# Layer 1: recurrent heads as a pipeline in slots, between the levels of one head the scan of the head before and the projections of the next

## The chip, the core and the metric

The kernel runs on one core of a Trainium2 chip. Five engines work from queues of their own, each in order: PE (matrix products; its weight loads are listed as PEld), DVE and ACT (element-wise work), POOL (a little arithmetic, and output DMAs) and SP (most input DMAs). The metric is the device time of one execution in microseconds, and lower is better. Before the change it was 3807.29 us, the median of three runs (3806.28 to 3817.9).

## The reference

The model has two layers over 1024 latent tokens and 256 context tokens, with 1024 features. Layer 0 (neighbourhood attention beside an mLSTM) isn't touched by the change. Layer 1 is a gated linear recurrence with 16 heads that runs forward and backward over the tokens. Cut to what matters:

```
q, f_fwd, f_bwd, i, z = split(h @ w_in)           # per head 128 columns of each
f = lb + (1 - lb) * sigmoid(f_pre)                # decay, per key feature; k = 1 - f
for d in (forward, backward):                     # i is the value
    S = final state over the 256 context tokens
    for each chunk of tokens:                     # b = running sum of log f in the chunk
        o += (q * exp(b)) @ S + (pairs t >= s: q_t . exp(b_t - b_s) k_s) @ i
        S = exp(b_last) * S + (k * exp(b_last - b))^T @ i
y = (rms(o_fwd + o_bwd) * h_norm * silu(z)) @ w_out
x = x + gate * y
```

All of it is in 32-bit floats. The large products are made of three matmuls with operands that were split into a high and a low part.

## The kernel before

**Stages of layer 1.** First `q_plain` and `q_seven` compute the values `i` and the gated `z` of all heads for the latent tokens (eight blocks of 256 columns) and write them to DRAM (`vzd`). Then the 16 heads follow, in a loop at the end of `build`. Then the output projection (`out_ahead`, `out_tile`).

**One head**, in the order in which the program is written:

- `hg_intra`. From the decay F and the query q come K = 1 - F and Q = q F, for two halves of 512 tokens. Then `hg_level` runs seven times on each half: blocks of 1, 2, 4 to 64 tokens are joined in pairs. A level copies the keys that it needs (`gksel`, ACT, L1022), makes 4 products of 128 x 128 (L1031, eight matmuls, since a 32-bit product takes two), puts the result into the matrix A under a mask (L1041, DVE), and multiplies K and Q by the decay of the neighbouring block (L1049, DVE, four times). At level 0 A is made anew (L1037), and `hg_diag` adds the diagonal. At the end K is transposed into `gkn` (L1006, L1008).
- `hg_vz` loads v and z of the head (SP), projects the values of the context tokens (24 matmuls of 256 columns, L120 to L122) and transposes them (L947).
- `hg_ctx` makes the two states after the context: running products of the decay (L960, L961, DVE), keys, transposes (L967), products (L974).
- `hg_scan` takes eight chunks of 128 tokens: seven backward states (L1071, L1073), then for each chunk three products into the accumulator bank (L1083 to L1085) and the next forward state (L1088, L1090); after four chunks each the norm and the gate (L1099, POOL for the inverse root, L1103).
- `hg_proj` of the **next** head: for both directions the context tokens and two halves of the latents through the decay weights (24 matmuls each; sigmoid L786 on ACT, affine step L787 on DVE), then q (L795, L796).
- `hg_y` transposes the output and writes it to DRAM (POOL).

**What sets the order.** Loops are unrolled in Python. A planner orders the instructions of each engine ahead of time: of what it holds ready at a moment it takes what stands first in the program, so what comes later in the program fills in where earlier work waits. Tiles are given out by tag from a fixed number of buffers, and an instruction waits until a buffer of its tag is free. What matters here: `gF` (decay of a half) has two buffers, and level 0 is the last to read it; `gFc` (decay of the context) has one; `gEc` has one, and both the context values of `hg_vz` and the running products of `hg_ctx` take it; `gq` has two, for the two halves of q and the keys of `hg_ctx`; the split weights have four slabs, two for each block of 128 columns. Of the eight PSUM banks two serve projections (`mm`), two transposes (`tr`), three small products (`s`), and one the scan (`acc`).

Of the kernel before, what the change touches and what calls it, by code (L numbers as in the profile page):

```python
# [18 lines left out]
P = 128  # L19
# [24 lines left out]
class Prog:  # L44
# [727 lines left out]
    def hg_proj(self, h, pool):  # L772
        nc, a = self.nc, self.a
        st = {}
        col = lambda i: a["wc"][:, i * 2048 + h * P : i * 2048 + (h + 1) * P]
        lb, olb = self.lb[:, 0, h : h + 1], self.lb[:, 1, h : h + 1]
        F = [self.t(pool, [P, 2, 512], F32, "gF", 2) for _ in range(2)]
        Fc = self.t(pool, [P, 2, CTX], F32, "gFc", 1)
        todo = [(d, t0, n) for d in range(2) for t0, n in ((LAT, CTX), (512, 512), (0, 512))]
        w = [None, None]  # L780
        for d, t0, n in todo:
            w[d] = w[d] or self.wring([col(1 + d)], P)
# [3 lines left out]
            nc.scalar.activation(dst, ps, AF.Sigmoid)  # L786
            nc.vector.tensor_scalar(out=dst, in0=dst, scalar1=olb, scalar2=lb, op0=ALU.mult, op1=ALU.add)  # L787
        q = {}
        w = self.wring([col(0)], P)
        for t0 in (512, 0):  # L790
            ps = self.ps("mm", [P, 512])
            self.proj_tr(ps, w, 0, t0, 512)
            q[t0 // 512] = self.t(pool, [P, 512], F32, "gq", 2)
            sg = self.t(pool, [P, 512], F32, "gsg", 1)
# [39 lines left out]
    def q_raw(self, pool, j):  # L834
        nc, raw = self.nc, {}
        for n in ("11", "21", "12", "22"):
# [95 lines left out]
    def hg_vz(self, h, st, pool):  # L932
        nc, a = self.nc, self.a
        v = self.t(pool, [P, NT, P], F32, "gv", 2)
        z = self.t(pool, [P, NT - 2, P], F32, "gz", 2)
        for t, i in ((v, 0), (z, 1)):
            nc.sync.dma_start(
                out=t[:, 0:8, :], in_=self.vzd[i, :, h * P : (h + 1) * P].rearrange("(c p) f -> p c f", p=P)
            )
# [8 lines left out]
        nc.scalar.copy(v[:, 8:10, :], pt)  # L948
        st["v"], st["z"] = v, z


    def hg_ctx(self, st, pool):
        nc = self.nc
        Fc, v = st["Fc"], st["v"]
        E = self.t(pool, [P, 2, CTX], F32, "gEc", 1)
        k = self.t(pool, [P, 2, CTX], F32, "gq", 2)
# [5 lines left out]
        nc.vector.tensor_scalar(out=k, in0=Fc, scalar1=-1.0, scalar2=1.0, op0=ALU.mult, op1=ALU.add)  # L962
        nc.vector.tensor_tensor(out=k, in0=k, in1=E, op=ALU.mult)
        p = self.ps("tr", [P, 4, P])
        for d in range(2):
            for j in range(2):
                nc.tensor.transpose(p[:, 2 * d + j, :], k[:, d, j * P : (j + 1) * P], self.ident)  # L967
        kn = self.t(pool, [P, 4, P], F32, "gknc", 1)
        nc.scalar.copy(kn, p)
        S = []  # L970
        for d in range(2):
            u = self.ps("s", [P, P])
            for j in range(2):
                nc.tensor.matmul(u, lhsT=kn[:, 2 * d + j, :], rhs=v[:, 8 + j, :], start=(j == 0), stop=(j == 1))  # L974
# [500 lines left out]
```

## Time and profile before

| | |
|---|---|
| median of three runs | 3807.29 us |
| profiled execution | 3808.09 us, span 3806.3 us |
| mean granted PE clock | 0.982 |
| busy: PE / DVE / ACT / POOL | 94% / 63% / 39% / 14% of the span |
| value and gate products of layer 1 | about 1975 to 2306 us from the span's start |
| heads of layer 1 | 2313 to about 3664 us |
| from K of one head to K of the next | 80 to 84 us, 64.8 for the first |
| output projection | to the end |

The profile's page gives for each engine the time in which it was busy. PE's matmuls overlap, so the duration of one is longer than the distance to the next. In the tables by stretch stands the busy time of each engine between two points of time, and behind it the number of instructions. A row of the order of time has the start, the time taken, engine, line, operation, written and read tiles, and in square brackets the idle time before it and what ended it. A row of groups has count, busy time and mean duration in ns, then the idle time before. A row of waits has who waited for whom, the total in us, how many times, and the longest.

### The profile page before, as it was taken

The page shows a single profiled execution, that of the slowest core. Times are in us where ns is not written, and L with a number is a line of the kernel's source. Part 1 is how long each engine was busy: PE and PEld are TensorE (multiplying, and loading weights), DVE is VectorE, ACT ScalarE, POOL GpSimd, SP SyncE. Part 2 cuts the span into 40 slices and gives each one's busy share as a digit, 9 for nine tenths or more (in the row PEclk, how much of TensorE's full clock was granted, in tenths as well). Part 3 has the DMA queues.
Part 4 walks back from the last instruction along what each step waited for, and adds up shares of the span by engine and source line. Part 5 has one row for each costly group of instructions (what it writes and reads, how often), then busy time and mean ns, then how long its engine had stood idle before and what let it go on. Part 6 is the DMA issues. An engine that isn't in the chain of part 4 may idle for free.

```text
span 3806.3 us, 65773 instructions
## 1 busy us (share of the span) xinstructions
PE 3575.2 (94%) x24618; PEld 3221.9 (85%) x24618; DVE 2383.2 (63%) x6294; ACT 1477.0 (39%) x3459; POOL 514.8 (14%) x880
## 2 busy tenths in 40 slices
PE   8999999999999999988879999899999899998989
PEld 5889999999999999976559998778888778887777
DVE  5546676666546556545448665766667766667763
ACT  5545555554434334333343332333333333333431
POOL 2222222222111122010011220000000000000000
PEclk9999999999999999999999999999999999999999
DMA  6522323232343343246233322111111111111244
GB/s 211 171 72 77 87 83 86 68 84 80 86 152 99 118 138 112 72 153 201 91 108 104 109 92 83 43 39 45 50 51 51 39 39 46 50 54 47 89 152 128
DMA packets 363054, 348.26 MB, mean 91 GB/s; under 512 B 31128, under 2 KB 315992, under 8 KB 362608
## 3 DMA queue, kind: packets, MB, share of 16 engines
q1 hardware_dynamic: 324560, 243.66, 21.9%
q0 software_dynamic: 38176, 100.40, 7.6%
q8 instruction: 195, 3.19, 0.3%
q14 instruction: 123, 1.01, 0.1%
HBM read 267.70 MB, written 76.08 MB: 90 GB/s over the span
## 4 chain that ended last, share of the span: by engine, by line
PE 62%; issue 14%; DVE 11%; DMA 7%; POOL 3%; ACT 2%; SPq 0%; POOLq 0%; ACTq 0%; DVEq 0%
PE mm L120 13%; PE mm L122 13%; PE mm L121 13%; DMA wraw<-yd 3%; DVE gQ L1049 3%; DVE gA L1041 3%; DVE gK L1049 2%; PE s L1031 2%; PE acc L677 2%; PE tr L657 2%; POOL vzd L883 2%; PE s L470 1%; PE acc L461 1%; PE mm L731 1%; PE mm L733 1%
## 5 line engine op out<-in xcount | busy, mean ns | idle before, releaser
L122 PE MATMUL mm<-wh,hl 128*128 128x256 f32 x2560 | 749.3, 293 | 0.3 <-DVE hl L253 0.3
L120 PE MATMUL mm<-wh,hh 128*128 128x256 f32 x2560 | 746.8, 292 | 0.0
L121 PE MATMUL mm<-wl,hh 128*128 128x256 f32 x2560 | 745.6, 291 | 0.0
L120 PE MATMUL mm<-hh,wh 128*128 128x512 f32 (+1 forms) x1344 | 487.6, 363 | 24.6 <-ACT gFc L786 16.8
L122 PEld LDWEIGHTS mm<-wh,hl 128*128 128x128 f32 x2560 | 488.8, 191 | 11.2 <-issue 4.1
L120 PEld LDWEIGHTS mm<-wh,hh 128*128 128x128 f32 x2560 | 489.0, 191 | 7.7 <-issue 1.4
L121 PEld LDWEIGHTS mm<-wl,hh 128*128 128x128 f32 x2560 | 489.0, 191 | 7.1 <-issue 0.8
L121 PE MATMUL mm<-hl,wh 128*128 128x512 f32 (+1 forms) x1344 | 485.3, 361 | 0.0
L122 PE MATMUL mm<-hh,wl 128*128 128x512 f32 (+1 forms) x1344 | 485.0, 361 | 0.0
L1031 PE MATMUL s<-gQ,gksel 128*128 128x128 f32 x1536 | 240.9, 303 | 74.4 <-ACT gksel L1022 61.6
L120 PEld LDWEIGHTS mm<-hh,wh 128*128 128x128 f32 x1344 | 255.7, 190 | 61.6 <-ACT gFc L786 19.7
L71 ACT CAST wh<-wraw 128x512 fp32r<-128x512 f32 x278 | 171.1, 620 | 335.6 <-PE mm L121 242.9
L1031 PEld LDWEIGHTS s<-gQ,gksel 128*128 128x128 f32 x1536 | 212.4, 201 | 95.9 <-ACT gksel L1022 73.7
L72 DVE TENSOR_TENSOR wl<-wraw,wh 128x512 fp32r<-128x512 f32 x278 | 189.9, 689 | 152.1 <-ACT wh L71 149.7
L122 PEld LDWEIGHTS mm<-hh,wl 128*128 128x128 f32 x1344 | 255.7, 190 | 34.6
L121 PEld LDWEIGHTS mm<-hl,wh 128*128 128x128 f32 x1344 | 255.8, 190 | 33.7
L731 PE MATMUL mm<-woh,yh 128*128 128x512 f32 x524 | 216.2, 413 | 55.6 <-ACT yh L71 38.2
L1022 ACT COPY gksel<-gK 128x512 f32<-128x512 f32 x224 | 148.7, 664 | 234.5 <-DVE gA L1041 94.3
L733 PE MATMUL mm<-woh,yl 128*128 128x512 f32 x524 | 215.5, 412 | 0.4 <-DVE yl L72 0.4
L732 PE MATMUL mm<-wol,yh 128*128 128x512 f32 x524 | 211.3, 404 | 0.0
L731 PEld LDWEIGHTS mm<-woh,yh 128*128 128x128 f32 x524 | 101.1, 193 | 90.7 <-ACT yh L71 55.9
L71 ACT CAST yh<-wraw 128x512 fp32r<-128x512 f32 x144 | 86.7, 619 | 217.4 <-DMA wraw<-yd 123.8
(432 smaller groups left out, 7900.5 us busy)
## 6 DMA issues: line engine op xcount, KB each, us to landing
wraw<-yd SPq DMA_DIRECT2D x144, 256.0 KB
wraw<-in_wc_dram SPq DMA_DIRECT2D x132, 256.0 KB
wraw<-in_wab_dram SPq DMA_DIRECT2D x112, 256.0 KB
md<-ev POOLq DMA_DIRECT2D x100, 256.0 KB, 2.8
adar<-in_wada_dram POOLq DMA_DIRECT2D x32, 512.0 KB, 4.6
b<-in_wc_dram SPq DMA_DIRECT2D x64, 256.0 KB
vzd<-qo POOLq DMA_DIRECT2D x128, 128.0 KB, 2.2
adar<-in_wada_dram SPq DMA_DIRECT2D x16, 512.0 KB
```

What stands on the lines that cost most here:

```text
L71: nc.scalar.copy(hi, x)
L72: nc.vector.tensor_tensor(out=lo, in0=x, in1=hi.bitcast(F32), op=ALU.subtract)
L120: mm(ps, lhsT=lh(k), rhs=rh(k), start=(k == 0), stop=False)
L121: mm(ps, lhsT=lh(k), rhs=rl(k), start=False, stop=False)
L122: mm(ps, lhsT=ll(k), rhs=rh(k), start=False, stop=(k == nk - 1))
L731: mm(ps, lhsT=yh[:, k, :], rhs=w.h(kk), start=(kk == 0), stop=False)
L732: mm(ps, lhsT=yh[:, k, :], rhs=w.l(kk), start=False, stop=False)
L733: mm(ps, lhsT=yl[:, k, :], rhs=w.h(kk), start=False, stop=(kk == 8 * len(qs) - 1))
L1022: nc.scalar.copy(ksel.rearrange("p (b s i) -> p b s i", s=2, i=h), pick(K))
L1031: nc.tensor.matmul(pa[:, c, :].rearrange("p (b s i) -> p b s i", s=2, i=h), lhsT=ksel[:, c * P : (c + 1) * P], rhs=qp[:, c * nbc : (c + 1) ...
L1041: nc.vector.copy_predicated(A, self.lmask[:, lev - 1, :].unsqueeze(1).to_broadcast([P, 4, P]), pa)
L1049: nc.vector.tensor_tensor(out=t[:, i, :, s, :], in0=t[:, i, :, s, :], in1=bc(tot), op=ALU.mult)
```

## The change

- **Slots.** `hg_intra` calls eight slots: slot 0 before level 0, slot i + 1 behind level i. `hg_scan` no longer runs, it returns its seven parts (three with backward states, four with two chunks each), and `hg_parts` (formerly `hg_proj`) returns the projections in parts. During the levels of head h the slots hold the scan of head h - 1 (slots 0 to 6), the context step of head h (slot 1), the projections of head h + 1 (decay in slots 2 to 5, context tokens last in slots 3 and 5, q in slots 6 and 7), the output of head h - 2 (slot 2) and the loads of v and z of head h (slot 4).
- **Tiles.** The context values and keys get tags of their own (`gvT`, `gvc`), `hg_ctx` makes its keys in place, and Q, A and the last decay products get four buffers, since two heads are alive.
- **Engines.** The affine step of the decay goes from DVE to ACT; half of the `gkn` copies goes from ACT to DVE; at level 6 two ACT copies of blocks stand in for the predicated copy; the copy of Q ahead of the product moves from level 6 to level 0.
- **Before the heads.** The first decay weights of head 0 are loaded while the value pool is still open. In `q_plain` only one half of the first weights is loaded early, and eight accumulators are kept open: first the products of the upper half of the features for all eight row tiles, then those of the lower half.

The diff, with `...` where lines are left out:

```diff
...
-    def hg_proj(self, h, pool):
+    def hg_parts(self, h, pool, w=None):
...
+        st, w, F = {"q": {}}, w or {}, {}
+
+        def weights(i):
+            if i not in w:
+                w[i] = self.wring([col(i)], P)
+            return w[i]
+
+        def f(d, t0, n):
+            if t0 not in F:
+                F[t0] = self.t(pool, [P, 2, n], F32, "gFc" if t0 == LAT else "gF", 1 if t0 == LAT else 2)
             ps = self.ps("mm", [P, n])
-            self.proj_tr(ps, w[d], 0, t0, n)
-            dst = Fc[:, d, :] if t0 == LAT else F[t0 // 512][:, d, :]
+            self.proj_tr(ps, weights(1 + d), 0, t0, n)
+            dst = F[t0][:, d, :]
             nc.scalar.activation(dst, ps, AF.Sigmoid)
-            nc.vector.tensor_scalar(out=dst, in0=dst, scalar1=olb, scalar2=lb, op0=ALU.mult, op1=ALU.add)
...
+            nc.scalar.activation(dst, dst, AF.Identity, scale=olb, bias=lb)
+            st["F"] = [F.get(0), F.get(512)]
+
+        def q(t0):
             ps = self.ps("mm", [P, 512])
...
-            nc.scalar.activation(sg, ps, AF.Sigmoid)
-            nc.vector.tensor_tensor(out=q[t0 // 512], in0=sg, in1=ps, op=ALU.mult)
-        return dict(F=F, Fc=Fc, q=q)
+            self.proj_tr(ps, weights(0), 0, t0, 512)
+            t = st["q"][t0 // 512] = self.t(pool, [P, 512], F32, "gq", 2)
+            nc.scalar.activation(t, ps, AF.Sigmoid)
+            nc.vector.tensor_tensor(out=t, in0=t, in1=ps, op=ALU.mult)
+
+        def c():
+            st["S"] = self.hg_ctx(F[LAT], weights(3), pool)
+
+        todo = [[]] + [[(f, d, 512, 512)] if k == 0 else [(f, d, 0, 512), (f, d, LAT, CTX)] for d in range(2) for k in range(2)]
+        todo += [[(q, 512)], [(q, 0)]]
+        st["c"] = c
+        return st, [[lambda x=x: x[0](*x[1:]) for x in xs] for xs in todo]
...
-            w = early if early and not z else [self.q_form(raw, f"{k}{z + 1}") for k in (1, 2)]
-            for c in (4, 0):
-                for i in range(4):
-                    ps = self.ps("sa", [P, 256])
-                    for k in range(2):
-                        self.q_mul(ps, self.q_h(c + i, k), w[k], k == 0, k == 1)
-                    self.q_out(pool, c + i, j, z, ps)
+            ps = []
+            w = early if not z else self.q_form(raw, "12")
+            for i in [4, 5, 6, 7, 0, 1, 2, 3]:
+                ps.append((i, self.q_ps()))
+                self.q_mul(ps[-1][1], self.q_h(i, 0), w, True, False)
+            w = self.q_form(raw, "22" if z else "21")
+            for i, p in ps:
+                self.q_mul(p, self.q_h(i, 1), w, False, True)
+                self.q_out(pool, i, j, z, p)
...
     def hg_vz(self, h, st, pool):
...
+        for n, i in (("v", 0), ("z", 1)):
+            st[n] = self.t(pool, [P, 8, P], F32, "g" + n, 2)
+            self.nc.sync.dma_start(
+                out=st[n], in_=self.vzd[i, :, h * P : (h + 1) * P].rearrange("(c p) f -> p c f", p=P)
             )
-        w = self.wring([a["wc"][:, 3 * 2048 + h * P : 3 * 2048 + (h + 1) * P]], P)
+
+    def hg_ctx(self, Fc, w, pool):
+        nc = self.nc
         ps = self.ps("mm", [P, CTX])
         self.proj_tr(ps, w, 0, LAT, CTX)
-        vT = self.t(pool, [P, CTX], F32, "gEc", 1)
+        vT = self.t(pool, [P, CTX], F32, "gvT", 1)
...
-        nc.scalar.copy(v[:, 8:10, :], pt)
-        st["v"], st["z"] = v, z
...
+        v = self.t(pool, [P, 2, P], F32, "gvc", 1)
+        nc.scalar.copy(v, pt)
         E = self.t(pool, [P, 2, CTX], F32, "gEc", 1)
-        k = self.t(pool, [P, 2, CTX], F32, "gq", 2)
...
-        nc.vector.tensor_scalar(out=k, in0=Fc, scalar1=-1.0, scalar2=1.0, op0=ALU.mult, op1=ALU.add)
-        nc.vector.tensor_tensor(out=k, in0=k, in1=E, op=ALU.mult)
+        nc.vector.scalar_tensor_tensor(out=E, in0=Fc, scalar=1.0, in1=E, op0=ALU.subtract, op1=ALU.mult)
...
         kn = self.t(pool, [P, 4, P], F32, "gknc", 1)
-        nc.scalar.copy(kn, p)
+        nc.scalar.activation(kn, p, AF.Copy, scale=-1.0)
...
-            s = self.t(pool, [P, P], F32, f"gS{d}", 10 if d else 2)
+                nc.tensor.matmul(u, lhsT=kn[:, 2 * d + j, :], rhs=v[:, j, :], start=(j == 0), stop=(j == 1))
+            s = self.t(pool, [P, P], F32, f"gSc{d}", 2)
...
-    def hg_intra(self, st, pool):
+    def hg_intra(self, st, pool, slots):
...
-            Q = self.t(pool, [P, 2, n], F32, "gQ", 2)
+            Q = self.t(pool, [P, 2, n], F32, "gQ", 4)
...
-            A = self.t(pool, [P, 4, P], F32, "gA", 2)
+            A = self.t(pool, [P, 4, P], F32, "gA", 4)
...
+        slot(0)
         for lev in range(7):
             for hf in (1, 0):
                 self.hg_level(hv[hf], lev, pool)
             if lev == 0:
                 for hf in (1, 0):
                     self.hg_diag(hv[hf], st["q"][hf], pool)
+            slot(lev + 1)
...
-                nc.scalar.copy(k_, p)
+                (nc.vector.tensor_copy if d else nc.scalar.copy)(k_, p)
                 H["kn"].append(k_)
...
-        if lev == 6:
+        if lev == 0:
...
+        elif lev == 6:
+            nc.scalar.copy(A[0:64, :, 64:128], pa[0:64, :, 64:128])
+            nc.scalar.copy(A[64:128, :, 0:64], pa[64:128, :, 0:64])
         else:
             nc.vector.copy_predicated(A, self.lmask[:, lev - 1, :].unsqueeze(1).to_broadcast([P, 4, P]), pa)
...
-    def hg_scan(self, h, st, halves, S, pool):
+    def hg_scan(self, st, halves, pool):
...
+        S = {0: st["S"][0]}
+        sb = {7: st["S"][1]}
+        o4 = {}
+
+        def state(d, c, old, tag, bufs):
...
+            nc.tensor.matmul(u, lhsT=H["kn"][d][:, c % 4, :], rhs=v[:, c, :], start=True, stop=True)
+            s = self.t(pool, [P, P], F32, tag, bufs)
...
+            return s
+
+        def back(c):
+            sb[c - 1] = state(1, c, sb[c], "gS1", 9)
+
+        def ahead(c):
...
-            nc.tensor.matmul(o, lhsT=H["Q"][:, 1, cs], rhs=Sf, start=False, stop=True)
+            nc.tensor.matmul(o, lhsT=H["Q"][:, 1, cs], rhs=S[c], start=False, stop=True)
...
+                S[c + 1] = state(0, c, S[c], "gS0", 2)
+            if c % 4 == 3:
...
+        do = lambda f, *cs: [lambda c=c: f(c) for c in cs]
+        return [do(back, 7, 6, 5), do(back, 4, 3), do(back, 2, 1)] + [do(ahead, c, c + 1) for c in (0, 2, 4, 6)]
...
-                early = []
-                for k in range(2):
-                    rows = a["wc"][k * 512 : (k + 1) * 512, 3 * 2048 : 3 * 2048 + 256]
-                    early.append(self.wblock(self.wp, "w", [rows], 4, 256, op, ring=self.slabs))
+                early = self.wblock(self.wp, "w", [a["wc"][0:512, 3 * 2048 : 3 * 2048 + 256]], 4, 256, op, ring=self.slabs)
...
-                self.nq = 0
+                self.nq = -1
...
+                    first = [a["wc"][:, 2048 : 2048 + P]]
+                    early = {1: self.wblock(self.wp, "w", first, KD, P, [pool, 4, "b11"], ring=self.slabs)}
...
-                st = self.hg_proj(0, pool)
+                st, parts = self.hg_parts(0, pool, early)
+                for part in sum(parts, []):
+                    part()
+                scan, done = [], [None, None]
                 for h in range(16):
-                    hv = self.hg_intra(st, pool)
-                    self.hg_vz(h, st, pool)
-                    S = self.hg_ctx(st, pool)
-                    self.hg_scan(h, st, hv, S, pool)
-                    done = st
-                    if h < 15:
-                        st = self.hg_proj(h + 1, pool)
-                    self.hg_y(h, done, pool, self.yd2)
+                    nxt, parts = self.hg_parts(h + 1, pool) if h < 15 else (None, [])
+                    slots = [[] for _ in range(8)]
+                    for i, x in enumerate(scan):
+                        slots[i] += x
+                    slots[1] += [st["c"]]
+                    for i, x in enumerate(parts):
+                        slots[i + 1] += x
+                    if h > 1:
+                        slots[2].append(lambda h=h, st=done[0]: self.hg_y(h - 2, st, pool, self.yd2))
+                    slots[4].append(lambda h=h, st=st: self.hg_vz(h, st, pool))
+                    hv = self.hg_intra(st, pool, slots)
+                    scan = self.hg_scan(st, hv, pool)
+                    done, st = [done[1], st], nxt
+                self.hg_y(14, done[0], pool, self.yd2)
+                for part in sum(scan, []):
+                    part()
+                self.hg_y(15, done[1], pool, self.yd2)
```

More of the change, by code (lines that the diff above doesn't have):

```diff
@@ L835, in q_raw @@
         nc, raw = self.nc, {}
-        for n in ("11", "21", "12", "22"):
+        for n in ("11", "21", "12", "22")[j == 0 :]:
             c0 = (3 if n[1] == "1" else 4) * 2048 + j * 256
@@ L984, in hg_intra, with slot @@
         hv = {}
+        def slot(i):
+            for part in slots[i]:
+                part()
         for hf in (1, 0):
@@ L1097, in hg_scan @@
-            jk = self.t(pool, [P, P], F32, "gjk", 1)
-            for i in range(4):
-                nc.scalar.activation(jk, o4[:, i, :], AF.Square, accum_out=ss[:, i : i + 1])
-            self.rsqrt(ss, ss, 1.0 / P)
-            for i in range(4):
-                zi = z[:, c - 3 + i, :]
-                nc.vector.scalar_tensor_tensor(
-                    out=zi, in0=o4[:, i, :], scalar=ss[:, i : i + 1], in1=zi, op0=ALU.mult, op1=ALU.mult
-                )
+                S[c + 1] = state(0, c, S[c], "gS0", 2)
@@ new lines, in ahead @@
+            if c % 4 == 3:
+                ss = self.t(pool, [P, 4], F32, "gss", 2)
+                jk = self.t(pool, [P, P], F32, "gjk", 1)
+                for i in range(4):
+                    nc.scalar.activation(jk, o4[0][:, i, :], AF.Square, accum_out=ss[:, i : i + 1])
+                self.rsqrt(ss, ss, 1.0 / P)
+                for i in range(4):
+                    zi = z[:, c - 3 + i, :]
+                    nc.vector.scalar_tensor_tensor(
+                        out=zi, in0=o4[0][:, i, :], scalar=ss[:, i : i + 1], in1=zi, op0=ALU.mult, op1=ALU.mult
+                    )
```

51 lines of the change are left out of this document (6 added, 45 removed).

## The prediction

> **What bounds the kernel now.** I read the page first (engine shares, then the chain that ended last), then a table of busy time by stretch, then the order of time inside one head, then the waits.
>
> ```profile
> PE 3575.2 (94%) x24618; PEld 3221.9 (85%) x24618; DVE 2383.2 (63%) x6294; ACT 1477.0 (39%) x3459; POOL 514.8 (14%) x880
> PE 62%; issue 14%; DVE 11%; DMA 7%; POOL 3%; ACT 2%; SPq 0%; POOLq 0%; ACTq 0%; DVEq 0%
> ```
>
> PE is the engine to look at, but its 94% hides holes: matmuls overlap, so a sparse PE also looks busy. The stretches below show them. Columns: length, then busy time (and instructions) of PE, PEld, DVE, ACT, POOL, then the granted clock, DMA share and GB/s. 2403 to 3541 is the stretch of 14 heads of layer 1 (heads 1 to 14), 81.3 us each; 2729 to 2810 is one head.
>
> ```profile
> 2403.00:3541.00 1138.00, 1033.70 (x6414) 918.38 (x6413) 782.23 (x1960) 372.92 (x798) 51.20 (x84) 0.98 0.15 46
> 2729.00:2810.00 81.00, 73.54 (x460) 65.77 (x459) 55.90 (x141) 26.63 (x57) 3.65 (x6) 0.98 0.16 46
> 2655.00:2699.00 44.00, 44.00 (x287) 40.20 (x285) 26.52 (x66) 13.82 (x34) 3.65 (x6) 1.00 0.27 78
> 2699.00:2721.00 22.00, 14.51 (x108) 12.51 (x106) 21.91 (x57) 8.40 (x15) 0.00 (x0) 1.00 0.00 1
> 3596.00:3638.00 42.00, 42.00 (x240) 36.63 (x239) 30.56 (x69) 19.14 (x34) 0.12 (x1) 1.00 0.25 76
> ```
>
> In a head, 44 us are solid (PE 44.00 of 44) and then 22 us aren't: PE 14.51, DVE 21.91 of 22. In those 22 us the levels run alone:
>
> ```profile
> 2705.60 0.97 PEld L1031 LDWEIGHTS s<-gQ,gksel 128*128 128x128 f32 x8 [0.98 <-ACT gksel L1022]
> 2705.64 1.13 PE L1031 MATMUL s<-gQ,gksel 128*128 128x128 f32 x8 [0.82 <-ACT gksel L1022]
> 2706.09 0.71 DVE L1041 COPY_PREDICATED gA<-glm,s 128x512 f32<-128x512 uint8 x1
> 2706.70 0.73 DVE L1049 TENSOR_TENSOR gQ<-gQ,gT 128x256 f32<-128x256 f32 x2
> 2706.84 0.62 ACT L1022 COPY gksel<-gK 128x512 f32<-128x512 f32 x1 [1.33 <-DVE gA L1041]
> 2707.37 0.74 DVE L1049 TENSOR_TENSOR gK<-gK,gT 128x256 f32<-128x256 f32 x2
> 2707.55 0.97 PEld L1031 LDWEIGHTS s<-gQ,gksel 128*128 128x128 f32 x8 [0.98 <-ACT gksel L1022]
> ```
>
> A half-level comes every 1.95 us (2705.60 to 2707.55), paced by DVE; PE has 0.97 us of loads in it and stands 0.98. No projection fills the gap, and this is why:
>
> ```profile
> 2719.47 0.38 PE L947 MATMUL tr<-ident,gEc 128*128 128x128 f32 x2
> 2719.91 0.68 DVE L960 TENSOR_TENSOR_SCAN gEc<-gFc,gzero 128x255 f32<-128x255 f32 x1
> 2720.51 0.67 DVE L961 TENSOR_TENSOR_SCAN gEc<-gFc,gzero 128x255 f32<-128x255 f32 x1
> 2721.20 0.66 ACT L786 ACTIVATE gFc<-mm 128x256 f32<-128x256 f32 x2 [0.68 <-DVE gEc L961]
> 2721.64 0.50 PE L120 MATMUL mm<-hh,wh 128*128 128x512 f32 x1 [1.13 <-ACT gFc L786]
> ACT gFc L786 <- DVE gEc L961: 12.8, 14, 1.3
> PE mm L120 <- ACT gFc L786: 15.7, 14, 1.1
> ```
>
> The next head's projection starts with its context part, whose tile gFc has one buffer. This head's context step still has to read that buffer (L960, L961); it writes gEc, a single buffer that holds the context values until their transposes (L947), and those run only when the levels are over. So the projection restarts behind the levels, in each of 14 heads (the last two rows: total us, times, longest).
>
> **PE's work in a head.** I price a matmul by the distance between starts in solid stretches, since its duration overlaps its neighbours.
>
> ```profile
> 2722.44 0.40 PE L120 MATMUL mm<-hh,wh 128*128 128x512 f32 x1
> 2725.87 0.39 PE L120 MATMUL mm<-hh,wh 128*128 128x512 f32 x1
> 2318.24 0.28 PE L120 MATMUL mm<-hh,wh 128*128 128x256 f32 x1
> 2318.96 0.28 PE L120 MATMUL mm<-hh,wh 128*128 128x256 f32 x1
> 2353.91 1.30 PEld L1031 LDWEIGHTS s<-gQ,gksel 128*128 128x128 f32 x8
> ```
>
> 15 matmuls of 512 columns lie between the first two: 0.229 us each. Six of 256 between the next two: 0.12. Of 128: eight loads in 0.97 us, the last lasting about 0.19, so 0.78 / 7 = 0.111; at level 0, where Q is read with a stride, 1.11 / 7 = 0.159 (last row). By the code a head has 144 matmuls of 512 (six projections of 24), 72 of 256 (three of 24) and 242 of 128, together 458 (the table counts 460 in 81 us). That is 144 x 0.229 + 72 x 0.12 + 242 x 0.111 = 33.0 + 8.6 + 26.9 = 68.5 us, plus 16 x 0.048 = 0.8 at level 0 now. PE idles 81.3 - 69.3 = 12 us a head, 168 us in 14 heads, nearly all in the levels.
>
> **The change, part by part.**
>
> Order. The context step moves to slot 1 with tiles of its own (gvT, gEc), so gFc is free two slots before the next head writes it (slot 3). Scan chunks of the head before, context step and projections of the next get places between levels. No matmul is added. What blocked the filler goes; after level 0 the two gF buffers free, and 39 us of projection (33.0 and two of 2.9) plus the scan can fill. How solid will PE be? The nearest row is 3596 to 3638, the last head, where the output projection is the filler among the levels; its largest groups:
>
> ```profile
> L732 PE MATMUL mm<-wol,yh 128*128 128x512 f32 x43 | 17.1, 399 | 0.0
> L1031 PE MATMUL s<-gQ,gksel 128*128 128x128 f32 x80 | 10.7, 276 | 0.0
> ```
>
> There are 131 matmuls of 512 (43, 43, 42 in the three lines of that sum, and 3) and 109 of 128 (80 here, 13 and 16): 30.0 + 12.1 = 42.1 us of work in 42. So it can be all but full. I take 97%, some 2 us a head for the seams between the parts: 68.5 / 0.97 = 70.6 us, 10.7 less a head, 14 x 10.7 = 150 us. Bounds: 99% gives 69.2 (169 us); below, no gain at all and a loss (rivals).
>
> Engines. The rows for what moves between them:
>
> ```profile
> L787 DVE TENSOR_SCALAR gF<-gF,lb 128x512 f32<-128x512 f32 x56 | 30.5, 545 | 107.4 <-ACT gF L786 107.4
> L786 ACT ACTIVATE gF<-mm 128x512 f32<-128x512 f32 x56 | 33.3, 595 | 20.9 <-PE mm L122 20.9
> L1114 ACT ACTIVATE gyt<-tr,hnc 128x512 f32<-128x512 f32 x28 | 19.3, 689 | 112.7 <-PE tr L1112 112.7
> L1041 DVE COPY_PREDICATED gA<-glm,s 128x512 f32<-128x512 uint8 x168 | 123.9, 738 | 4.5 <-PE s L1031 3.9
> L1008 ACT COPY gkn<-tr 128x512 f32<-128x512 f32 x56 | 31.6, 585 | 38.7 <-PE tr L1006 38.6
> L1037 DVE TENSOR_TENSOR gA<-s,glm 128x512 f32<-128x512 f32 x28 | 19.4, 692 | 50.4 <-PE s L1031 50.4
> ```
>
> The decay's affine step leaves DVE (4 x 0.545 a head, and two narrow ones, about 0.4) for ACT: a per-partition operand costs 0.689 - 0.595 = 0.094, so two make about 0.78 for 512 columns and 0.6 for 256 (estimates). Two of four gkn copies go to DVE (about 0.69 from PSUM, as L1037; ACT saves 0.585). At level 6 a predicated copy of 0.738 per half becomes two ACT copies of about 0.4. The Q copy moves from level 6 to level 0, one per half as before. The context's two DVE passes become one. DVE: 55.9 - 3.0 + 1.4 - 1.5 - 0.4 = 52.4 us a head. ACT: 26.6 + 4.3 - 1.2 + 1.6 + 0.5 = 31.8. Both stay under 70.6, so I charge nothing: the cover is PE's own work, and were it gone, DVE's 52.4 would be the floor. If ACT were late, gksel and then PE's levels wait behind it.
>
> DMA queues. Each head's gv and gz loads move on SP to slot 4, ahead of the next weights; gz waits for the output transposes of two heads earlier (slot 2), and weights queue behind. DMA share is 0.15, a whole slot lies between: 0. The output DMA of a head goes out on POOL one head later, and the scan's inverse root (POOL, slots 4 and 6) queues behind it, with the one accumulator bank behind that; POOL is busy 51.20 of 1138, so 0, at most 4 us at the end, where head 14's write now stands ahead of head 15's.
>
> Start of the heads, and the first value/gate block:
>
> ```profile
> 2309.45 1.47 SPq L100 DMA_DIRECT2D wraw<-in_wc_dram  x3
> 2312.35 1.28 ACT L71 CAST wh<-wraw 128x512 fp32r<-128x512 f32 x2 [5.99 <-DMA wraw<-in_wc_dram]
> 2313.03 0.58 PE L120 MATMUL mm<-hh,wh 128*128 128x256 f32 x1 [7.63 <-ACT wh L71]
> 2314.47 0.41 PE L122 MATMUL mm<-hh,wl 128*128 128x256 f32 x1
> 2316.18 0.37 PE L121 MATMUL mm<-hl,wh 128*128 128x256 f32 x1
> 1987.66 0.58 PE L863 MATMUL sa<-wh,hh 128*128 128x256 f32 x1 [4.62 <-ACT qo L878]
> ```
>
> The first decay weights are now loaded (two DMAs on SP) and split under the last gate product, so the 7.63 us wait goes. What is late next: the second weights, which can only be asked for where the first are now (2309.45, ready 2313); three projections, 13.8 us, cover that. Behind the wait 256-column matmuls start 0.21 apart (2314.47 to 2316.18, eight) instead of 0.12 up to 2316.4: 1.5 us more. Gain 9. In the first block only the k-half "11" is early; "21" must be loaded once the old pool is gone, near 1987, and takes 2.9 us from issue to cast (2309.45 to 2312.35) while PE already stands 4.62 there. Eight accumulators instead of four give PE no more to do before that. I charge 2 us, between -1 (two splits fewer ahead of the last row tile) and 5.
>
> The Trainium skill, "TensorE: Matmul & The Clock Gate", Part 1, says that an idle window of about 3.4 us halves PE's clock until a busy one has passed. The trace agrees: 2313.03 to 2316.4 is 3.4 us at the slow pace. By that rule the gain from closing the wait is 7.6 + 1.7 = 9.3 us, against my 9 from rows.
>
> The last head keeps its shape: levels among output filler, its scan exposed. 1 us from level 0.
>
> **Sum.** 150 + 9 - 2 + 1 = 158. The profiled execution took 3808.1 us (span 3806.3 and 1.8 around it), 0.8 above the median: 3808.1 - 158 = 3650, and against the median of 3807.3, 3649.
>
> The Trainium skill, "Perfetto Trace Analysis", section "Identifying the Most-Contended Engine", judges PE by weight-load busy time, not matmul busy time. Here that speaks against my price: a head's loads take 65.77 us, the solid stretches read 40.20 of 44 (91%), so by that measure a solid head takes 65.77 / 0.914 = 72.0, the gain is 14 x 9.3 + 8 = 138 and the time 3670. The trace agrees that matmul busy time says little: 44.00 of 44, and still 73.54 of 81 over a whole head.
>
> **Rivals.**
>
> A, a hole at each head's start. Level 0 needs fresh K, Q, A, sums and diagonal on DVE, eight or nine passes near 0.69 per half, about 13 us for two; PE has level 0 and diagonal (3.6), the context step (72 x 0.12 is 8.6 in all, 2.9 of it here, and 14 x 0.111) and five backward states there, some 9 us, and the next projection waits for gF. For: DVE waits 50.4 us before L1037 today. Against: the last q projection (5.5 us) lies there too. Price 4 to 6 us a head: 75.6, gain 14 x 5.7 + 8 = 88, time 3720.
>
> B, slower: queue order. PE takes its queue in order. Now 14 scan states join 14 half-levels between parts, each ending in a PE-DVE or PE-ACT-PE round; where the order written out leaves too little work between, the 0.98 us gap of today's half-level stays. It decides at 81.3 - 68.5 = 12.8 us, 13 such gaps of 28, plus a half more for the 9 us at the start. With 21 exposed: 89.1 us, 14 x 7.8 - 8 = 101 more, 3909. Against: 2655 to 2699 holds such scan states already, and PE is solid.
>
> C, the change doesn't do what it says: another single buffer (gF until level 0, or the four weight slabs) blocks the filler as gFc does. Only the start is gained: 3800. Against: both are freed a slot or more before use.
>
> **How the numbers follow.** Forecast (97% to 99%, down to 74 us a head) 0.66, A 0.17, C 0.04, B 0.13. Time 3649, own range 3620 to 3700. Leaving out B, C and the worse half of A leaves 3615 to 3735, about 0.75 to 0.8. About 0.3% (11 us) is what a measurement can tell from no change: faster 0.83, same 0.04, slower 0.13.
>
> **What would show it.** Right: distance between heads near 70.6 us; no PE wait on gFc; context transposes early in a head; PE near 99% busy, weight loads near 90% in the heads, PE's matmul count unchanged; DVE near 52 of 70; no 7.6 us wait before the first head. Wrong: PE waits on gksel, gS or gA of 0.5 to 1 us at many half-levels (B); one hole of several us per head near L1037 (A); waits on another tile's buffer at 22 us per head (C).

## The result, and the profile after

The changed kernel takes 3548.44 us (median of 4 runs, 3547.46 to 3549.17), the kernel before 3806.78 on the same chip: a ratio of 0.9315, 95% interval 0.9298 to 0.9333. That is 258 us less; I had forecast 158 less, and my own range began at 3620. The profiled execution took 3547.46 us with a span of 3545.7.

The engine shares and the chain that ended last, on the page of the changed kernel:

```profile
PE 3473.2 (98%) x24618; PEld 3175.5 (90%) x24618; DVE 2311.4 (65%) x6182; ACT 1550.8 (44%) x3587; POOL 538.4 (15%) x880
PE 83%; issue 8%; DMA 4%; DVE 2%; POOL 1%; ACT 1%; SPq 0%; POOLq 0%; ACTq 0%; DVEq 0%
```

The number of matmuls is the same (24618). What left the chain is above all DVE (11% to 2%) and "issue" (14% to 8%).

Busy time by stretch in the changed kernel (columns as in the prediction): the last part of layer 0's output stage, then heads 1 to 14, then one head.

```profile
1843.00:1913.00 70.00, 70.00 (x351) 58.98 (x350) 43.56 (x113) 39.01 (x104) 8.00 (x16) 1.00 0.41 125
2339.00:3301.00 962.00, 962.00 (x6403) 875.38 (x6402) 719.49 (x1851) 436.04 (x896) 71.33 (x80) 1.00 0.18 53
2613.00:2682.00 69.00, 69.00 (x461) 62.76 (x461) 51.78 (x135) 31.70 (x67) 5.36 (x6) 1.00 0.18 54
```

The heads are solid: PE 962.00 of 962. Inside a head, a piece of the context step, a half-level and a projection now stand next to each other. The timeline of the changed kernel (start, length, instruction, and in brackets the idle time before it; line numbers are those of the kernel shown, so the product of a level, L1031 before, is L1041 here, and the sigmoid and the affine step are L789 and L790):

```profile
2641.90 0.40 PE L122 MATMUL mm<-hh,wl 128*128 128x512 f32 x1
...
2642.13 1.06 PE L978 MATMUL s<-gvc,gknc 128*128 128x128 f32 x8
2642.33 0.60 ACT L789 ACTIVATE gF<-mm 128x512 f32<-128x512 f32 x1 [2.94 <-PE mm L122]
...
2642.95 0.48 PE L120 MATMUL mm<-hh,wh 128*128 128x512 f32 x1
2642.96 0.81 ACT L790 ACTIVATE gF<-gF,lb 128x512 f32<-128x512 f32 x1
...
2643.72 0.40 PE L120 MATMUL mm<-hh,wh 128*128 128x512 f32 x1
...
2643.95 0.77 PE L1041 MATMUL s<-gQ,gksel 128*128 128x128 f32 x5
```

No PE row has a bracket: the idle time of 0.8 to 1 us at each half-level is gone. Now ACT waits for PE (2.94). The last row is cut off by the end of the view, after five of its eight matmuls.

I cut both spans at the same four events: the last norm of layer 0, the last write of values and gates, the first K of head 1, and the first K of head 15.

| stretch | before, us | after, us | difference | forecast |
|---|---|---|---|---|
| to the last norm of layer 0 | 1978.8 | 1912.9 | -65.9 | in the next row |
| value and gate stage | 328.3 | 330.4 | +2.1 | +2 |
| to the first K of head 1 | 95.9 | 95.9 | 0 | -9 |
| heads 1 to 14 | 1138.0 | 961.4 | -176.6 | -150 |
| from the first K of head 15 to the end | 265.3 | 245.1 | -20.2 | -1 |

So the profiled execution lies 103 us below my sum, for three reasons: 66 us in a stage that the forecast did not look at, 27 us more in the heads, and 10 us more around them (20 against 9 and 1).

### The profile page after: what moved, and what is told of

The parts are those of the page before. It is cut to its first block, busy times and chain, and to the rows that moved or that the text cites. A ratio compares the mean times of both kernels' runs of the same rounds, so it can differ in the third digit from the quotient of the medians.

```text
span 3545.7 us, 65436 instructions
## 1 busy us (share of the span) xinstructions
PE 3473.2 (98%) x24618; PEld 3175.5 (90%) x24618; DVE 2311.4 (65%) x6182; ACT 1550.8 (44%) x3587; POOL 538.4 (15%) x880
## 4 chain that ended last, share of the span: by engine, by line
PE 83%; issue 8%; DMA 4%; DVE 2%; POOL 1%; ACT 1%; SPq 0%; POOLq 0%; ACTq 0%; DVEq 0%
PE mm L122 14%; PE mm L120 14%; PE mm L121 14%; PE s L1041 6%; PE acc L677 2%; PE tr L657 2%; PE mm L731 2%; PE mm L732 2%; PE mm L733 2%; PE sa L873 2%; PE sa L872 2%; PE sa L874 2%; PE s L470 1%; PE acc L461 1%; PE s L1086 1%
## 5 line engine op out<-in xcount | busy, mean ns | idle before, releaser
L731 PE MATMUL mm<-woh,yh 128*128 128x512 f32 x524 | 210.6, 403 | 16.3 <-issue 10.1
L733 PE MATMUL mm<-woh,yl 128*128 128x512 f32 x524 | 209.5, 400 | 0.0
L1041 PE MATMUL s<-gQ,gksel 128*128 128x128 f32 x1536 | 199.8, 276 | 0.0
L1041 PEld LDWEIGHTS s<-gQ,gksel 128*128 128x128 f32 x1536 | 192.4, 191 | 7.0
L145 POOL TENSOR_SCALAR gss<-gss 128x4 f32<-128x4 f32 x32 | 16.6, 518 | 968.0 <-ACT gjk L1111 968.0
L1062 DVE TENSOR_TENSOR gQ<-gQ,gT 128x256 f32<-128x256 f32 x384 | 143.1, 413 | 28.0 <-PE s L1041 28.0
```

The source lines that it names most:

```text
L731: mm(ps, lhsT=yh[:, k, :], rhs=w.h(kk), start=(kk == 0), stop=False)
L733: mm(ps, lhsT=yl[:, k, :], rhs=w.h(kk), start=False, stop=(kk == 8 * len(qs) - 1))
L1041: nc.tensor.matmul(pa[:, c, :].rearrange("p (b s i) -> p b s i", s=2, i=h), lhsT=ksel[:, c * P : (c + 1) * P], rhs=qp[:, c * nbc : (c + 1) ...
L1062: nc.vector.tensor_tensor(out=t[:, i, :, s, :], in0=t[:, i, :, s, :], in1=bc(tot), op=ALU.mult)
```

## Experiments

Each time is a median; "before" is the kernel before on the same chip. It took 3803.78 to 3806.78 us in the four sets of runs, so a difference of some 3 us between times of different sets says nothing.

### Where do 66 us of layer 0 come from?

In the kernel before, this is the same part of the output stage, 1853 to 1979, by busy time:

```profile
1853.00:1979.00 126.00, 100.42 (x432) 71.40 (x431) 54.14 (x127) 48.33 (x119) 8.66 (x19) 0.97 0.28 87
```

and by its waits (total us, times, longest):

```profile
ACT yh L71 <- DMA wraw<-yd: 49.0, 24, 3.7
PEld mm L731 <- ACT yh L71: 34.3, 24, 3.6
PE mm L731 <- ACT yh L71: 24.9, 24, 3.1
```

PE waits for ACT, and ACT for the rows of y. The timeline of the kernel before shows the round:

```profile
1900.85 0.62 ACT L71 CAST yh<-wraw 128x512 fp32r<-128x512 f32 x1 [3.60 <-DMA wraw<-yd]
...
1901.52 0.50 PE L731 MATMUL mm<-woh,yh 128*128 128x512 f32 x1 [0.90 <-ACT yh L71]
1902.21 0.36 SPq L718 DMA_DIRECT2D wraw<-yd  x1
...
1905.05 0.62 ACT L71 CAST yh<-wraw 128x512 fp32r<-128x512 f32 x1 [1.01 <-DMA wraw<-yd]
```

The next rows are asked for (1902.21) only when the last ones have been split, and are split themselves 2.8 us later: one staging buffer in use, though the tag `wraw` has three. The theory: the second early half of the first weights ("21") was requested ahead of this stage. Its two pieces sat in two of the three buffers, since their destinations, the slabs of tag `w`, were held by the last two pieces of the output weights until the stage's end. The timeline has both ends of this. The request (the last two of its three DMAs) and the split:

```profile
1780.82 1.60 SPq L100 DMA_DIRECT2D wraw<-in_wc_dram  x3
1974.60 1.31 ACT L71 CAST wh<-wraw 128x512 fp32r<-128x512 f32 x2 [2.71 <-PE mm L733]
```

For more than 190 us the two pieces held their staging buffers, until PE's last products of the stage (L733).

**The first block alone.** The kernel before with only the edit of the first value/gate block: one early half, and `q_raw`, `q_plain` and the first value of `nq` as in the changed kernel.

```diff
-                early = []
-                for k in range(2):
-                    rows = a["wc"][k * 512 : (k + 1) * 512, 3 * 2048 : 3 * 2048 + 256]
-                    early.append(self.wblock(self.wp, "w", [rows], 4, 256, op, ring=self.slabs))
+                early = self.wblock(self.wp, "w", [a["wc"][0:512, 3 * 2048 : 3 * 2048 + 256]], 4, 256, op, ring=self.slabs)
```

> The kernel before with the new first block of the value product alone: one early half instead of two, eight accumulators, products of the upper half of the features first. The heads are as before. My recorded step charged 2 us for this: 3809. The theory from the two traces is that this edit is what took 65.9 us from the end of layer 0 (last norm at 1978.8 us before, 1912.9 after) and gives 2 back in the value product: 3743, with ACT's waits for y rows (96.2 us in 44 waits before) falling to some 16. If those 65 us came from elsewhere (the heads' new tiles moving the pools), it stays near 3807.

Measured: 3741.36 against 3803.78, ratio 0.9837 (0.9823 to 0.9852). The last norm comes at 1910.6, and the stage is full:

```profile
1843.00:1911.00 68.00, 68.00 (x341) 57.27 (x340) 41.37 (x106) 37.92 (x102) 8.07 (x17) 1.00 0.39 120
```

The edit that I had priced at a cost of 2 us is worth 62.

**Is it the staging buffers, or the eight accumulators?** The kernel before, where only the second early half gets staging of its own:

```diff
-                    early.append(self.wblock(self.wp, "w", [rows], 4, 256, op, ring=self.slabs))
+                    early.append(self.wblock(self.wp, "w", [rows], 4, 256, [op, 2, "eraw"] if k else op, ring=self.slabs))
```

> The kernel before, still with both early halves and four accumulators, but the second half's two raw pieces get staging buffers of their own (a tag with two buffers). Staging theory: these pieces waited for slabs that the last two pieces of the output weights held, and kept two of the three buffers through which the rows of y come; with their own they keep none, and 55 to 65 us go: 3742 to 3752. Accumulator theory: what helped was that eight accumulators and one half let PE start the value product under the output stage; then this does nothing: 3804 to 3810.

Measured: 3743.27, ratio 0.984 (0.9826 to 0.9855). The same gain without the accumulators, with both halves still loaded early: the cause is the staging buffers.

**Does it add up?** The changed kernel with the early load and the first block as before (the diff of the first run, reversed):

> The changed kernel with the early load and the first value/gate block as they were before (two early halves, pairs of half sums in four accumulators). Theory (the staging edit is worth its 62 us by itself, whatever the heads do): 3548 + 62 = 3610, 3603 to 3617, with the last norm of layer 0 at about 1978. Rival (part of the 62 us is given back, since later stages then start with weights ready): 3560 to 3600.

Measured: 3609.92, 61.5 us slower than the changed kernel. The stage has its holes back, and the heads are as they were in the changed kernel:

```profile
1853.00:1979.00 126.00, 100.99 (x438) 71.20 (x437) 55.68 (x132) 49.59 (x124) 8.65 (x19) 0.99 0.29 91
2403.00:3365.00 962.00, 962.00 (x6403) 875.41 (x6402) 719.79 (x1851) 436.17 (x896) 71.33 (x80) 1.00 0.18 53
```

The staging edit and the heads are independent.

### What makes the heads solid: the tiles or the order?

**A tile of its own for the context values**, in the kernel before:

```diff
-        vT = self.t(pool, [P, CTX], F32, "gEc", 1)
+        vT = self.t(pool, [P, CTX], F32, "gvT", 1)
```

> The kernel before with one tag changed: the context values get a tile of their own (gvT) and no longer hold gEc. No slots, no pipeline, nothing moved in the program. Theory of the prediction (the single buffers gEc and gFc block the filler): the context's running products run early, gFc comes free, projections run among the levels; 69 to 73 us a head, 3807 - 14 x (81.3 - 71) = 3663, between 3635 and 3695. Rival (the order in slots is what matters): PE stays idle in the levels, 79 us a head or more, 3775 to 3807.

Measured: 3717.24, ratio 0.9774 (0.9758 to 0.979): between the two. A head takes 76.1 us. Its stretch of heads, and what PE waits for in it:

```profile
2396.00:3462.00 1066.00, 1037.42 (x6494) 929.03 (x6493) 789.85 (x1976) 371.92 (x804) 53.62 (x84) 0.98 0.17 50
```

```profile
PE s L1031 <- DVE gQ L991: 20.4, 25, 1.2
PE tr L1112 <- PE s L1031: 4.7, 14, 0.6
PE acc L1083 <- DVE gA L1041: 2.7, 10, 0.3
```

In the kernel before, PE's longest wait in these heads was another:

```profile
PE s L1031 <- ACT gksel L1022: 61.6, 75, 0.8
```

The waits on gksel and gFc are gone; a new one stands in their place. L991 makes Q of the next head, and its two buffers are read by the scan of this one until the end.

**Two buffers for gFc instead**, in the kernel before:

```diff
-        Fc = self.t(pool, [P, 2, CTX], F32, "gFc", 1)
+        Fc = self.t(pool, [P, 2, CTX], F32, "gFc", 2)
```

> The kernel before with a second buffer for gFc, the context still late. If gFc's one buffer is the block itself, this does as much as the separate gvT tile: 3635 to 3695. If the late context step costs of its own (its gEc, its keys in gq, its place behind the levels), it falls short by 2 us a head or more: above 3695. If neither buffer matters: 3800 or more.

Measured: 3797.36, ratio 0.9979 (0.997 to 0.9989), a gain of 0.2%. The projection does run among the levels now, but is then missing behind them, where the context step of the head still waits for `gEc`:

```profile
PE tr L967 <- DVE gq L963: 39.4, 13, 3.3
PE s L1031 <- DVE gQ L991: 16.3, 14, 1.2
PE s L1031 <- ACT gksel L1026: 13.1, 16, 1.8
```

So the tile that two steps of the context shared was the root, and the full gFc only its trace.

**Both pairs of tiles**, the kernel before with `gvT` and four buffers for Q and A:

```diff
-        vT = self.t(pool, [P, CTX], F32, "gEc", 1)
+        vT = self.t(pool, [P, CTX], F32, "gvT", 1)
...
-            Q = self.t(pool, [P, 2, n], F32, "gQ", 2)
+            Q = self.t(pool, [P, 2, n], F32, "gQ", 4)
...
-            A = self.t(pool, [P, 4, P], F32, "gA", 2)
+            A = self.t(pool, [P, 4, P], F32, "gA", 4)
...
-        Tn = self.t(pool, [P, 2, nb], F32, f"gT{lev}", 2)
+        Tn = self.t(pool, [P, 2, nb], F32, f"gT{lev}", 4 if lev == 6 else 2)
```

> The kernel before with a tile of its own for vT (as in the run that gave 3717 us, 76.1 us a head) and, in addition, four buffers instead of two for the levels' Q and A tiles (and for the last level's decay products). In that run PE waited 5.5 us in three heads for Q, which the scan of the head before still reads. Theory (two single or double buffers hold the heads back): a head takes 73.5 to 74.5 us, as in the changed kernel without slots, and the time is 3680 to 3695. Rival (the rest of that run's 76.1 is the order of the work): 75.5 to 76.1 us a head, 3708 to 3718.

Measured: 3667.34, ratio 0.9636 (0.9622 to 0.9651), better than either expectation. From head 2 on a head takes 72.1 to 72.2 us. Heads 1 to 14, and one head:

```profile
2392.00:3411.00 1019.00, 1003.34 (x6462) 901.96 (x6461) 783.82 (x1973) 366.25 (x802) 51.16 (x84) 1.00 0.17 52
2905.00:2977.00 72.00, 70.86 (x460) 63.70 (x459) 55.47 (x141) 25.87 (x58) 3.65 (x6) 1.00 0.18 52
```

The wait on Q is gone; what is left is small (11.0 us in 14 heads for A at level 0):

```profile
PE s L1031 <- DVE gA L1037: 11.0, 14, 0.8
PE mm L120 <- ACT gvT L944: 4.7, 13, 0.4
```

Four lines of tags and buffer counts, with the order of the program untouched, take the heads from 1138.0 to 1019.6 us: 118 of the 177.

**The tiles without the slots.** The changed kernel, with the program order of before:

```diff
-                    hv = self.hg_intra(st, pool, slots)
-                    scan = self.hg_scan(st, hv, pool)
+                    hv = self.hg_intra(st, pool, [[] for _ in range(8)])
+                    st["c"]()
+                    self.hg_vz(h, st, pool)
+                    for part in sum(self.hg_scan(st, hv, pool), []):
+                        part()
+                    for part in sum(parts, []):
+                        part()
+                    self.hg_y(h, st, pool, self.yd2)
```

> The changed kernel with the slots emptied: the program order of before (levels, context step, loads, scan, then the next head's projections, output), with all the new tiles, buffers, engine moves and the new start. Slot theory: separate tiles alone fill the levels but use up the filler there, as the run with the own gvT tile showed (76.1 us a head, holes now in the scan and at level 0), so 74 to 77 us a head: 3548 + 14 x (75.5 - 68.8) = 3642, between 3615 and 3665. Buffer theory: with four Q, four A and the context's own tiles the planner can run ahead by itself, whatever the program order: 69 to 70 us a head, 3548 to 3570.

Measured: 3599.88, ratio 0.946 (0.9446 to 0.9474), 73.7 us a head. The slots are worth 51 us beside the new tiles: 70 us in heads 1 to 14 (1031.4 us here), of which the changed kernel spends 16 ahead of them (the first K of head 1 comes at 2339.2, here at 2323.6). Its heads are 0.9 us longer than in the run before, in spite of fewer DVE passes. The waits show where: PE stands 31.4 us in heads 1 to 14 (15.7 in the run before), and 18.4 of it is a wait that the run before doesn't have, of the key transposes for ACT's copy of the context values:

```profile
PE tr L971 <- ACT gvc L960: 18.4, 12, 1.5
```

**The scan out of the slots.** The changed kernel; the context step and the projections stay between the levels, the scan runs in one piece behind them (and the output of a head one head earlier):

```diff
-                    for i, x in enumerate(scan):
-                        slots[i] += x
...
-                    scan = self.hg_scan(st, hv, pool)
+                    for part in sum(self.hg_scan(st, hv, pool), []):
+                        part()
```

> The changed kernel with only the scan taken out of the slots: the scan of a head runs in one piece behind its own levels, the context step and the projections of the next head stay between the levels. Theory (the scan's chain of PE and DVE rounds needs other work beside it, and the projections are then used up among the levels): 75 to 80 us a head, 3635 to 3705, slower than the 3600 without any slots. Rival (the planner fills the scan by itself, what counts is where the projections and the context step stand): 68.8 to 70.5 us a head, 3548 to 3575.

Measured: 3574.27, ratio 0.9391 (0.9377 to 0.9405), 70.5 us a head from head 3 on:

```profile
2340.00:3332.00 992.00, 977.97 (x6438) 882.72 (x6438) 738.05 (x1860) 439.90 (x918) 56.04 (x84) 1.00 0.18 55
2835.00:2905.00 70.00, 69.08 (x457) 62.31 (x456) 52.41 (x133) 31.09 (x65) 4.00 (x6) 1.00 0.18 53
```

My theory (that the scan would stand exposed, 75 to 80 us) falls. The time is at the upper end of the rival. The context step and the projections in slots (with the loads and the output of a head, which move too) bring 25.6 us (3599.88 to 3574.27), the scan in slots another 25.8.

### The small terms

**The affine step back on DVE**, in the changed kernel:

```diff
-            nc.scalar.activation(dst, dst, AF.Identity, scale=olb, bias=lb)
+            nc.vector.tensor_scalar(out=dst, in0=dst, scalar1=olb, scalar2=lb, op0=ALU.mult, op1=ALU.add)
```

> The changed kernel with the decay's affine step back on DVE (3.0 us a head more on DVE, about 4.3 less on ACT). My step: hidden under PE's work, so 3545 to 3552. If DVE's time in the levels matters after all, 1 to 3 us a head: 3562 to 3595.

Measured: 3542.96, ratio 0.9312 (0.9298 to 0.9326): by the two intervals no difference, though 2 us below the range that I expected. That the step runs on ACT gains nothing; on either engine PE's work covers it.

**The copy of Q back at level 6**, in the changed kernel:

```diff
-        if lev == 0:
+        if lev == 6:
```

> The changed kernel with the copy of Q back at level 6 instead of level 0. PE has no idle time in the heads now (69.00 busy of 69), so PE's strided read at level 0 should show in full: 16 x 0.048 = 0.8 us a head, 16 heads, 12 us: 3560. If some slack remains that hides it: 3546 to 3551.

Measured: 3557.53, ratio 0.935 (0.9336 to 0.9364): 9.1 us more, where I had expected 12. In the profiled executions heads 1 to 14 take 975.5 us against 961.4, 1.0 us a head where the price was 0.8, and the part behind them is 2.5 us shorter. So the strided read of Q isn't hidden on a PE that has no idle time.

**The first decay weights not loaded early**, in the changed kernel:

```diff
-                    first = [a["wc"][:, 2048 : 2048 + P]]
-                    early = {1: self.wblock(self.wp, "w", first, KD, P, [pool, 4, "b11"], ring=self.slabs)}
...
-                st, parts = self.hg_parts(0, pool, early)
+                st, parts = self.hg_parts(0, pool)
```

> The changed kernel without the early load of the first decay weights. My step: the 7.6 us wait and the slow clock behind it come back, 9 us: 3557. If the first head's other work would have covered it: 3548 to 3551.

Measured: 3558.92, ratio 0.9355 (0.9339 to 0.937), 10.5 us more. Its timeline:

```profile
2247.96 0.80 PE L120 MATMUL mm<-hh,wh 128*128 128x512 f32 x1 [7.71 <-ACT wh L71]
2248.55 0.63 PE L121 MATMUL mm<-hl,wh 128*128 128x512 f32 x1
2248.98 0.63 PE L120 MATMUL mm<-hh,wh 128*128 128x512 f32 x1
...
2252.82 0.63 PE L120 MATMUL mm<-hh,wh 128*128 128x512 f32 x1
2253.25 0.46 PE L121 MATMUL mm<-hl,wh 128*128 128x512 f32 x1
...
2255.15 0.39 PE L120 MATMUL mm<-hh,wh 128*128 128x512 f32 x1
2255.38 0.39 PE L122 MATMUL mm<-hh,wl 128*128 128x512 f32 x1
```

and two stretches of it (the granted clock is the third figure from the end):

```profile
2248.00:2253.00 5.00, 5.00 (x12) 3.95 (x13) 2.01 (x3) 1.24 (x2) 0.00 (x0) 0.50 1.04 302
2254.00:2260.00 6.00, 6.00 (x28) 4.97 (x27) 0.69 (x1) 1.94 (x3) 0.00 (x0) 1.00 0.64 189
```

A wait of 7.71 us, then a dozen matmuls 0.43 us apart (2248.55, 2248.98, and so on to 2253.25) where the later ones are 0.23 apart (2255.15, 2255.38): 12 x 0.2 = 2.4 us. The two together are 10.1 of the 10.5 us measured. The granted clock was 0.50 in the slow stretch and 1.00 behind it. The Trainium skill, "TensorE: Matmul & The Clock Gate", Part 1, says that the clock is halved after an idle window and comes back only after a busy one; the trace agrees (0.50, then 1.00). The slow pace lasted 5.3 us here, against 3.4 in the rows of the prediction.

**A faster version.** After the change one hole of PE is left at the start of the same output stage, where the first rows and the last weights share the staging buffers. ACT splits the weights that lie there only after the last work of the stage before (DVE `og`), and the first rows stand behind them. What PE and ACT wait for there in the changed kernel (1730 to 1913; "issue" means that the profile names nothing that PE waited for):

```profile
PE mm L731 <- issue: 10.1, 1, 10.1
...
ACT wh L71 <- DVE og L761: 10.1, 1, 10.1
ACT woh L71 <- DMA woraw<-in_woab_dram: 5.8, 7, 3.0
```

So: five staging buffers in that stage instead of three (`tt_raw` is true for that stage's pool alone), and the affine step on DVE.

```diff
-            yr = self.t(rp or yp, [P, 512], F32, "wraw", 3).rearrange("p (j t) -> p j t", j=4)
+            yr = self.t(rp or yp, [P, 512], F32, "wraw", 5 if tt_raw(self, rp or yp) else 3).rearrange("p (j t) -> p j t", j=4)
...
-                raws[:] = [op, 3, "wraw"]
+                raws[:] = [op, 5, "wraw"]; self.op0 = op
...
-                early = self.wblock(self.wp, "w", [a["wc"][0:512, 3 * 2048 : 3 * 2048 + 256]], 4, 256, op, ring=self.slabs)
+                early = self.wblock(self.wp, "w", [a["wc"][0:512, 3 * 2048 : 3 * 2048 + 256]], 4, 256, op, 5, ring=self.slabs)
```

> The changed kernel with the decay's affine step back on DVE (3543 us by itself) and five instead of three staging buffers in layer 0's last output stage. ACT waits 16.4 us for rows there, but PE is busy 70.00 of 70 us in that stage. If that wait is covered by PE's queue: 3541 to 3546, no change. If the rows still hold PE up at the stage's start: 3530 to 3540.

Measured: 3533.31, ratio 0.9282 (0.9266 to 0.9297), 10 us below the run with the affine step alone and 15 below the changed kernel. Where PE stood 10.1 us, it now has this wait:

```profile
PE mm L731 <- ACT yh L71: 2.5, 1, 2.5
```

## Why the prediction was wrong, and where it was right

**The first value/gate block: the step that failed.** Of the 103 us by which the sum fell short, 66 lie in the stage ahead of this block, and the term that the prediction had for it was a cost: "Eight accumulators instead of four give PE no more to do before that. I charge 2 us, between -1 (two splits fewer ahead of the last row tile) and 5." I asked when the half that is no longer early would arrive, and never what its early request had cost: two of three staging buffers for a whole stage. Measured: a gain of 62 us (two runs, one from each side), and 2.1 us more in the value stage. That these are the 2 us charged is partly luck: PE does wait for the late half (2.29 us at 1924.59), but the wait of 4.62 us that it had near this point before is gone, and what then makes the stage longer I didn't trace. The profile had it: I read the heads and the seams of the diff, and not the waits of the stage in which the removed request stood. In that stretch PE was 100.42 of 126 us busy, and the waits named `wraw`.

**The heads: right mechanism, size too small.** "I take 97%, some 2 us a head for the seams": there are no seams. The priced work was 68.5 us a head, and a head takes 68.7: 99.7%. In the 14 heads the view of waits has no row for PE at all. 14 x 12.6 = 177 us instead of 150. The start-to-start price of the matmuls was the right one. By weight-load time (the Trainium skill, "Perfetto Trace Analysis", "Identifying the Most-Contended Engine") I had worked out 72.0 us a head. The runs don't bear that out: the 460 loads of a head read 65.77 us in the kernel before and 62.76 now, so that busy time isn't a fixed amount of work either.

**What blocked the filler** was named right, gFc held up by `gEc`, and the chip showed the order of cause: a second gFc buffer brings 0.2%, another tag for the values 2.3%. But the step was incomplete. I credited the order ("Scan chunks of the head before, context step and projections of the next get places between levels") with the gain; two thirds of it come with tags and buffer counts alone, for the planner already moves projections among the levels when their tiles are free. The slots, with the rest of the edits that go with them, give the last third.

**Start and end.** The early load: forecast 9, measured 10.5. The start as cut in the table shows nothing of it, because PE has done 64 matmuls more by that point. The stretch from the last write of values and gates to the first K of head 1, in the kernel before:

```profile
2307.00:2403.00 96.00, 86.29 (x495) 75.80 (x496) 55.78 (x127) 28.61 (x50) 0.54 (x1) 0.96 0.25 71
```

and in the changed kernel:

```profile
2243.00:2339.00 96.00, 96.00 (x559) 84.70 (x558) 58.52 (x140) 40.33 (x68) 0.54 (x1) 1.00 0.25 75
```

That work is then missing in the last part, which has some 55 matmuls fewer and is 20 us shorter where I had 1. At 0.229 us a matmul that is at most 13 us (an estimate); the rest I didn't trace. Of that stretch's gain some 13 us come with the buffer counts too (252.5 us from the first K of head 15 to the end in the run with `gvT` and four Q and A). I had said that the last head keeps its shape.

**Engines.** DVE 51.8 and ACT 31.7 us a head against 52.4 and 31.8 forecast, and hidden, as the affine step on DVE shows. The affine pass on ACT takes 0.81 us; I had estimated 0.78.

**Rivals.** A (a hole of 4 to 6 us at each head's start): none, PE 69.00 of 69. B (queue order, slower): no half-level leaves a gap. C (another single buffer blocks the filler): not in the changed kernel, but it is exactly what the run with `gvT` alone met, with Q in two buffers.

## What to carry to other kernels

A load asked for early holds its staging buffer until its destination is free: when a diff moves or drops a request, read the waits of the stage in which it stood, not only of the one that uses it. Before a loop's order is rewritten by hand, give each tile that blocks the filler another tag or buffer, one at a time, and look which wait takes the place of the one removed; here that gave two thirds of the gain in the heads. Where enough independent work is at hand, price a PE-bound loop by the distance between the starts of its matmuls, and allow little for seams.

## What the runs showed of the chip

After a wait of 7.71 us, matmuls of 512 columns stood 0.43 us apart for 5.3 us (granted clock 0.50) and then 0.23 apart (1.00); this hole on PE cost 10.1 us, a third more than its own length.
